# Heads' probabilities turned by transposing transfers of 2-byte halves instead of products with the unit matrix

## The chip, the cores and the metric

The kernel runs on one core of a Trainium2 chip. Five engines work side by side, each through its own queue of instructions in order: TensorE (PE; its weight loads are listed apart as PEld), VectorE (DVE), ScalarE (ACT), GpSimd (POOL) and SyncE (SP), which here only issues transfers. They wait for each other through semaphores. The metric is the device time of one execution in microseconds (us); the median of the runs shown counts.

## The reference

A trunk of two layers over 256 tokens of width 2048, batch 1, all in float32: a Mamba-2 layer, then a sparse-attention layer, each followed by `x <- LayerNorm(alpha * x + mixer(x))`. The change lies in the second layer, in the attention of its 32 heads:

```python
c_q, c_kv, k_idx, w_idx, gate = jnp.split(proj, [s1, s2, s3, s4], -1)
q = (c_q @ w_uq).reshape(b, L, DSA_N_HEADS, DSA_HEAD_DIM)
q_lat = jnp.einsum('bthd,hcd->bthc', q, w_uk)
...
_, sel = lax.top_k(score, k_top)                  # 64 of up to 256 keys for each token
kv_sel = jax.vmap(lambda c, i: c[i])(c_kv, sel)
logits = jnp.einsum('bthc,btkc->bthk', ql, kv_sel) * attn_scale
logits = jnp.where(valid[:, :, None, :], logits, -jnp.inf)
pr = jax.nn.softmax(logits, -1)
return jnp.einsum('bthk,btkc->bthc', pr, kv_sel)  # then: @ w_uv per head, * silu(gate), @ w_out
```

The kernel does not gather. It makes full keys and values of each head (`k`, `v`), adds a mask `mb` that drops the keys outside the chosen 64, and takes the softmax over all causal keys.

## The kernel before

Weights come in units of 128x1024 float32 (512 KB). `Stream.load` lets SP load one into one of four `raw` buffers; `Stream.convert` and `finish` split it into a rounded part `hi` (ACT, L120) and a rest `lo` (DVE, L144), again four buffers each, three to four units ahead of PE; each product on PE is then done as hi*hi + hi*lo + lo*hi. `Stream.run` sets the order of everything: for each unit it emits the conversion of a later one, the unit's own products on PE, and then one step of every active side job. A side job is a Python generator, and each `yield` ends its step for this unit. A step that stands k yields after another is thus k units later in every engine's queue; the tile pools add the waits that buffers and data need.

The heads' stage takes two heads (a pair `p`) after each other from units `pair_a` (keys and values, L956 to L967) and `pair_b` (queries, L978 to L980), with one or two gate products of two units each in between (L336, `g`). `head_steps(h)` is the side job of one head. Token rows lie on the 128 partitions, in two halves, and only causal blocks are kept, so a head's scores are 128x384: a first block of 128 for the earlier half and 256 for the later. Its steps, one unit each:

1. four products of queries and keys into `pl` (L1016 to L1019)
2. DVE adds the mask, scales and takes the row maximum (L1027) into `lg`
3. ACT takes the exponential and the row sum (L1032)
4. DVE divides by the sum (L1035, L1037)
5. nothing
6. PE turns the three 128x128 blocks of `lg` with `ident` into PSUM, `pt` (L1043)
7. ACT copies the first 256 columns, rounded, into `ph` (L1049) and the last 128 into `p2` (L1050); DVE takes the rest `pl` (L1051)
8. nothing
9. PE multiplies values and turned probabilities (L1055 to L1058)
10. to 12. DVE multiplies with the gate into `og` (L1061), then ACT and DVE split it (L1068, L1070)

`lg` and `og` have two buffers each. A period of the stage is ten units with four heads: two units lie between one head's start and the next, three times, and then four. `cmask` is a 128x384 mask that the first layer used; `par` holds per-channel parameters, whose first 256 columns the first layer used. GpSimd does no arithmetic in the heads' stage.

Of the kernel before, what the change touches and what calls it, by code (L numbers as in the profile page):

```python
# [9 lines left out]
F32 = mybir.dt.float32  # L10
F32R = mybir.dt.float32r
I32 = mybir.dt.int32
AF = mybir.ActivationFunctionType
ALU = mybir.AluOpType
PSUM = bass.MemoryType.PSUM

P = 128
T = 256
# [51 lines left out]
class Stream:  # L70
# [30 lines left out]
    def convert_halves(self, i):  # L101
# [3 lines left out]
        for k in range(2):  # L105
            c = slice(k * 512, (k + 1) * 512)
            self.nc.scalar.activation(h[:, c], r[:, c], AF.Copy)
            self.nc.vector.tensor_sub(l[:, c], r[:, c], h[:, c].bitcast(F32))
        self.ready += 1

    def convert(self, i, eng, later=False):

        if i < len(self.units):
# [4 lines left out]
            if u.use in (KEYS, TWO):  # L118
                r = r.rearrange("p (a b) -> p a b", a=2)
            self.nc.scalar.activation(h, r, AF.Copy)  # L120
            self.halfway[i] = l, r, h.bitcast(F32)
# [56 lines left out]
def trunk_kernel(ctx: ExitStack, tc: tile.TileContext, x, xt, w1, wdt, dtp, prm, wo1,  # L178
                 wkv, wcq, wix, wg, wab, wo2, lnr, out):
    nc = tc.nc  # L180
# [18 lines left out]
    def y_tile(name):  # L199
        return p_y.tile([P, 512], F32, tag="y", name=name)  # L200

    def m_tile(name):
        return p_m.tile([P, 512], F32, tag="m", name=name)
# [9 lines left out]
    par = cpool.tile([P, PC_N], F32, tag="par", name="par")  # L213
# [3 lines left out]
    ident = cpool.tile([P, P], F32, tag="ident", name="ident")  # L217
    make_identity(nc, ident)
    cmask = cpool.tile([P, 384], F32, tag="cmask", name="cmask")
# [6 lines left out]
    def rsqrt(pool, dst, val, n, w, tag):  # L226

        t = pool.tile([n, w], F32, tag=tag, name=tag)
        v.tensor_scalar(dst.bitcast(I32), val.bitcast(I32), -0.5, MAGIC, op0=ALU.mult,
                        op1=ALU.add)  # L230
# [5 lines left out]
    def rsqrt1_steps(dst, val, t):  # L236

        v.tensor_scalar(dst.bitcast(I32), val.bitcast(I32), -0.5, MAGIC1, op0=ALU.mult,
                        op1=ALU.add)
# [35 lines left out]
    def dt_steps():  # L275
# [3 lines left out]
        da, acs = (scr[0:NH1, 6144 + T * k:6144 + T * (k + 1)] for k in range(2))  # L279
        nc.scalar.activation(x0, p_dt[:, 0:P], AF.Identity, bias=dtb[:, 0:1])  # L280
        nc.scalar.activation(an, dtb[:, 1:2], AF.Exp)
        v.scalar_tensor_tensor(e, x0, -1.0, x0, op0=ALU.mult, op1=ALU.min)
        v.tensor_scalar_mul(an, an, -1.0)
        nc.scalar.activation(e, e, AF.Exp)
        v.tensor_scalar_add(s, e, 2.0)
# [99 lines left out]
    def conv_steps(g, kind, ci, cc, cell):  # L385
# [4 lines left out]
        def w(k):  # L390
            return convh[:, cc * 5 + k:cc * 5 + k + 1]
        nc.scalar.activation(acc, ps, AF.Identity, scale=w(3), bias=w(4))
        yield
# [187 lines left out]
    for g in range(NG):  # L581
        for kind, n in (("B", 1), ("C", 1), ("x", 4), ("z", 4)):
            for ci in range(n):
# [5 lines left out]
                for half in range(2):  # L589
                    k = len(st.units)  # L590
# [420 lines left out]
    def head_steps(h):  # L1011
        p, k = divmod(h, 2)
        (qh, ql, q1), (kh, kl, k1) = ([a[:, k, :] for a in PR[p][nm]] for nm in "qk")
        vh, vl, v2 = (a[:, k * P:(k + 1) * P] for a in PR[p]["v"])
        pl = y_tile(f"lg{h}")
        nc.tensor.matmul(pl[:, 128:384], qh, kh, start=True, stop=False)  # L1016
        nc.tensor.matmul(pl[:, 128:384], qh, kl, start=False, stop=False)
        nc.tensor.matmul(pl[:, 128:384], ql, kh, start=False, stop=True)
        nc.tensor.matmul(pl[:, 0:128], q1, k1, start=True, stop=True)  # L1019
        yield  # L1020
        lg = d2.tile([P, 384], F32, tag="lg", name=f"lgs{h}")
        mx = d2.tile([P, 2], F32, tag="mx", name=f"mx{h}")
        sm = d2.tile([P, 2], F32, tag="sm", name=f"sm{h}")
        rn = d2.tile([P, 2], F32, tag="rn", name=f"rn{h}")
        parts = ((0, 0, 128), (1, 128, 384))
        for j, a, b in parts:
            v.tensor_tensor_reduce(out=lg[:, a:b], in0=pl[:, a:b], in1=mb[:, a:b],  # L1027
                                   scale=-ATT_SCALE, scalar=3.0e38, op0=ALU.add, op1=ALU.min,
                                   accum_out=mx[:, j:j + 1])
        yield  # L1030
        for j, a, b in parts:
            nc.scalar.activation(lg[:, a:b], lg[:, a:b], AF.Exp, scale=-1.0,  # L1032
                                 bias=mx[:, j:j + 1], accum_out=sm[:, j:j + 1])
        yield
        v.reciprocal(rn, sm)  # L1035
        for j, a, b in parts:
            v.tensor_scalar(lg[:, a:b], lg[:, a:b], rn[:, j:j + 1], 0.5,  # L1037
                            op0=ALU.mult, op1=ALU.mult)
        yield
        yield  # L1040
        pt = m_tile(f"pt{h}")
        for a in (0, 128, 256):
            nc.tensor.transpose(pt[:, a:a + 128], lg[:, a:a + 128], ident)  # L1043
        yield
        if h == 0:
            d2.tile([P, 48], F32, tag="gap3", name="gap3", bufs=1)
        ph, pl = (d2.tile([P, T], F32R, tag=f"prT{j}", name=f"prT{h}_{j}") for j in range(2))
        p2 = d2.tile([P, P], F32, tag="prT2", name=f"prT{h}_2")
        nc.scalar.activation(ph, pt[:, 0:T], AF.Copy)  # L1049
        nc.scalar.activation(p2, pt[:, T:384], AF.Copy)  # L1050
        v.tensor_sub(pl, pt[:, 0:T], ph.bitcast(F32))  # L1051
        yield
        yield
        po = y_tile(f"o{h}")
        nc.tensor.matmul(po[:, 0:T], vh, ph, start=True, stop=False)  # L1055
        nc.tensor.matmul(po[:, 0:T], vh, pl, start=False, stop=False)
        nc.tensor.matmul(po[:, 0:T], vl, ph, start=False, stop=False)
        nc.tensor.matmul(po[:, P:T], v2, p2, start=False, stop=True)  # L1058
        yield
        og = d2.tile([P, T], F32, tag="og", name=f"og{h}")  # L1060
        v.tensor_mul(og, po[:, 0:T], GT.pop(h))  # L1061
        if h == 0:
            OG.append(big.tile([P, KT, 2 * T], F32R, tag="A", name="og0"))
        if h == 16:
            OG.append(big.tile([P, KT, 2 * T], F32R, tag="C", name="og1"))
        dst = OG[h // 16][:, h % 16, :]
        yield
        nc.scalar.activation(dst[:, 0:T], og, AF.Copy)  # L1068
        yield
        v.tensor_sub(dst[:, T:2 * T], og, dst[:, 0:T].bitcast(F32))  # L1070
        yield
# [3 lines left out]
    for p in range(NH2 // 2):  # L1075
        src = wab[2 * p]
        i = st.add(wab[2 * p], 1024, pair_a(p), KEYS)
        st.side(i, (evac_steps, p, ("k", "v")))
        i = st.add(wab[2 * p + 1], 1024, pair_b(p), STILL)
        st.side(i, (evac_steps, p, ("q",)))  # L1080
        if p == 0:
            st.extra[i + 1] = 64
        st.side(i + 3, (head_steps, 2 * p))
        st.side(i + 5, (head_steps, 2 * p + 1))
        n = (left * (p + 1)) // 16 - (left * p) // 16
        for _ in range(n):
            add_gate(next(gates))
# [146 lines left out]
    d2 = L["d2"] = heads.enter_context(tc.tile_pool(name="d2", bufs=2))  # L1234
# [110 lines left out]
    for i in range(len(st.units) - 4, len(st.units)):  # L1345
        st.homes[i] = wmore, 0
    wturn = ctx.enter_context(tc.tile_pool(name="wturn", bufs=1))
    turned = [[cqT[:, n, :], (cqT[:, 3, :], ckvT[:, 0, :], ckvT[:, 1, :])[n]]
              for n in range(3)] + [wturn.tile([P, P], F32R, tag="idr", name="idr")]
# [95 lines left out]
```

## Time and profile before

| | |
|---|---|
| median of 3 runs | 1222.63 us (1221.64 to 1222.91) |
| the profiled execution | 1221.88 us, its span 1219.9 us |
| granted TensorE clock, mean | 0.999 |
| heads' stage (797 to 1053 us of the span) | 256 us |
| transposes of the heads (L1043) | 96, from 797.0 to 1050.1 us |
| weight loads (L98) | 512 KB each, landing 3.5 to 4.0 us after issue (medians) |

A row of the timeline reads: start, duration, engine, line, operation, output <- inputs, sizes, count. A row of groups gives count, busy time, mean nanoseconds of one. Matmuls are pipelined, so the durations of neighbours overlap; the chain of waits counts each stretch of time once.

### The profile page before, as it was taken

What the parts mean: (1) busy time and instruction counts of PE and PEld (TensorE: products, weight loads), DVE (VectorE), ACT (ScalarE), POOL (GpSimd) and SP (SyncE); (2) the same over time, 40 slices, a digit from 0 to 9 for tenths busy, and PEclk for the clock granted to TensorE, in tenths of its full rate; (3) what the DMA queues carried; (4) which work ended last, traced back from release to release, by engine and by line L of the source; (5) the groups of instructions that cost most, each with busy time, mean ns of one, the idle gap of its engine ahead of it and who ended that gap; (6) DMA issues with size and microseconds to landing.
All of it is one profiled execution on the core that took longest, in us unless ns stands there. A gap on an engine that the chain in (4) does not pass through costs nothing.

```text
span 1219.9 us, 22898 instructions
## 1 busy us (share of the span) xinstructions
PE 1213.8 (99%) x8983; PEld 1132.3 (93%) x8983; DVE 907.1 (74%) x1651; ACT 670.8 (55%) x1178; POOL 71.2 (6%) x109
## 2 busy tenths in 40 slices
PE   9999999999999999999999999999999999999998
PEld 8999999999999999788888899999999999888886
DVE  6978788898888788757457768867777777566467
ACT  5555555666566556444346655566666666434341
POOL 0001011101110110110000000000000001000000
PEclk9999999999999999999999999999999999999999
DMA  8656656576656665566556564655544455876662
GB/s 299 217 200 187 207 189 205 166 228 194 201 171 226 195 196 178 194 246 220 190 191 200 202 206 153 178 159 165 159 160 152 156 161 193 314 230 184 198 192 100
DMA packets 65628, 236.78 MB, mean 194 GB/s; under 512 B 8024, under 2 KB 8160, under 8 KB 65136
## 3 DMA queue, kind: packets, MB, share of 16 engines
q1 hardware_dynamic: 60608, 215.29, 53.7%
q0 software_dynamic: 4912, 20.02, 5.1%
q8 instruction: 71, 1.16, 0.4%
q14 instruction: 37, 0.30, 0.1%
HBM read 231.00 MB, written 4.28 MB: 193 GB/s over the span
## 4 chain that ended last, share of the span: by engine, by line
PE 98%; DMA 1%; DVE 0%; issue 0%; SPq 0%; ACT 0%; DVEq 0%
PE acc L336 35%; PE g L336 14%; PE o L615 9%; PE o L617 9%; PE o L616 9%; PE y L494 2%; PE q L978 1%; PE q L979 1%; PE q L980 1%; PE pt L1043 1%; DMA scr<-in_xt_dram 1%; PE k L956 1%; PE k L957 1%; PE k L958 1%; PE v L967 1%; PE v L965 1%
## 5 line engine op out<-in xcount | busy, mean ns | idle before, releaser
L144 DVE TENSOR_TENSOR lo<-raw,hi 128x1024 fp32r<-128x1024 f32 (+1 forms) x400 | 489.1, 1225 | 256.6 <-ACT hi L120 256.2
L120 ACT ACTIVATE hi<-raw 128x1024 fp32r<-128x1024 f32 (+1 forms) x400 | 418.2, 1051 | 209.1 <-PE o L617 154.6
L336 PE MATMUL acc<-xT,hi 128*128 128x256 f32 (+1 forms) x2496 | 301.2, 277 | 0.0
L336 PEld LDWEIGHTS acc<-xT,hi 128*128 128x128 f32 x2496 | 291.1, 188 | 2.5 <-ACT E L447 1.2
L336 PE MATMUL acc<-xT,lo 128*128 128x256 f32 (+1 forms) x1248 | 156.6, 277 | 0.0
L336 PEld LDWEIGHTS acc<-xT,lo 128*128 128x128 f32 x1248 | 148.2, 188 | 0.1
L336 PE MATMUL g<-x1T,hi 128*128 128x256 f32 (+1 forms) x1024 | 126.4, 278 | 0.0
L336 PEld LDWEIGHTS g<-x1T,hi 128*128 128x128 f32 x1024 | 120.4, 188 | 0.2
L615 PE MATMUL o<-hi,yg 128*128 128x512 f32 x256 | 100.3, 392 | 0.0
L615 PE MATMUL o<-hi,og 128*128 128x512 f32 (+1 forms) x256 | 99.7, 389 | 0.0
L617 PE MATMUL o<-hi,yg 128*128 128x512 f32 x256 | 99.7, 389 | 0.0
L616 PE MATMUL o<-lo,yg 128*128 128x512 f32 x256 | 99.6, 389 | 0.0
L617 PE MATMUL o<-hi,og 128*128 128x512 f32 (+1 forms) x256 | 98.9, 386 | 0.0
L616 PE MATMUL o<-lo,og 128*128 128x512 f32 (+1 forms) x256 | 98.8, 386 | 0.0
L336 PE MATMUL g<-x1T,lo 128*128 128x256 f32 x512 | 70.2, 281 | 0.0
L396 DVE SCALAR_TENSOR_TENSOR ca<-acc,par,ca 128x255 f32<-128x255 f32 x138 | 66.2, 479 | 3.3
L336 PEld LDWEIGHTS g<-x1T,lo 128*128 128x128 f32 x512 | 62.9, 188 | 0.2
L403 ACT ACTIVATE xs<-ca 128x256 f32<-128x256 f32 x32 | 13.4, 419 | 83.0 <-DVE ca L396 49.5
L615 PEld LDWEIGHTS o<-hi,yg 128*128 128x128 f32 x256 | 48.1, 188 | 10.3 <-issue 0.2
L617 PEld LDWEIGHTS o<-hi,yg 128*128 128x128 f32 x256 | 48.0, 188 | 9.9
L616 PEld LDWEIGHTS o<-lo,yg 128*128 128x128 f32 x256 | 48.1, 188 | 9.8
L617 PEld LDWEIGHTS o<-hi,og 128*128 128x128 f32 x256 | 48.0, 188 | 9.8
(296 smaller groups left out, 1744.1 us busy)
## 6 DMA issues: line engine op xcount, KB each, us to landing
raw<-in_w_dram SPq DMA_DIRECT2D x160, 512.0 KB, 4.0
raw<-in_wo_dram SPq DMA_DIRECT2D x128, 512.0 KB, 4.0
raw<-in_wg_dram SPq DMA_DIRECT2D x64, 512.0 KB, 3.5
raw<-in_wab_dram SPq DMA_DIRECT2D x32, 512.0 KB, 3.8
abc<-acs_d POOLq DMA_DIRECT2D x32, 256.0 KB, 4.5
raw<-in_wcq_dram SPq DMA_DIRECT2D x8, 512.0 KB, 4.4
raw<-in_wkv_dram SPq DMA_DIRECT2D x8, 336.0 KB, 3.0
scr<-in_xt_dram SPq DMA_DIRECT2D x4, 512.0 KB, 6.9
```

Source lines behind the costliest of these rows:

```text
L120: self.nc.scalar.activation(h, r, AF.Copy)
L144: eng.tensor_sub(*self.halfway.pop(i))
L336: nc.tensor.matmul(ps[:, 0:n], wt, xs[:, kt, c * T:c * T + n], start=(kt == 0 and not lo and c == 0), stop=last and c == (1 - lo), skip_gr ...
L396: v.scalar_tensor_tensor(acc[:, d:], ps[:, :T - d], w(k), acc[:, d:], op0=ALU.mult, op1=ALU.add)
L403: nc.scalar.activation(dst, acc, AF.Tanh)
L494: nc.tensor.matmul(py[ks, c * T + s * P:(c + 1) * T], xsT[:, s, c, ks], ms[c][k][:, ws], start=(c == 0 and s == 0), stop=(s == 1), skip_gr ...
L615: nc.tensor.matmul(ps, ah, hs, start=(kk == 2 * first), stop=False)
L616: nc.tensor.matmul(ps, ah, ls, start=False, stop=False)
L617: nc.tensor.matmul(ps, al, hs, start=False, stop=(kk == 31))
L956: nc.tensor.matmul(ps, h[:, 0, o:o + P], ckvT[:, ct, 0:T], start=(ct == 0), stop=False)
L957: nc.tensor.matmul(ps, h[:, 0, o:o + P], ckvT[:, ct, T:2 * T], start=False, stop=False)
L958: nc.tensor.matmul(ps, l[:, 0, o:o + P], ckvT[:, ct, 0:T], start=False, stop=(ct == 1))
```

## The change

Steps 4 to 7 of a head turn the probabilities in another way. A 4-byte word is seen as two 2-byte halves (`bitcast(U16)`). After DVE's division, GpSimd copies `lg` into `cmask` with all low halves first and all high halves behind them (384 each), and SP issues one `dma_start_transpose` that turns the six 128x128 blocks of halves into a new tile `ptu`. Two units later GpSimd joins the halves of the first 256 columns to words, `pt` in SBUF; a unit after that ACT and DVE read these as they read PSUM before, and ACT joins the last 128 columns itself, into a piece of `par`. `ptu` and `ptf` have one buffer, `cmask` is one, and `og` has one buffer instead of two.

```diff
         for j, a, b in parts:
             v.tensor_scalar(lg[:, a:b], lg[:, a:b], rn[:, j:j + 1], 0.5,
                             op0=ALU.mult, op1=ALU.mult)
-        yield
-        yield
-        pt = m_tile(f"pt{h}")
-        for a in (0, 128, 256):
-            nc.tensor.transpose(pt[:, a:a + 128], lg[:, a:a + 128], ident)
+        halves = cmask.bitcast(U16)
+        turned = d2.tile([P, 768], U16, tag="ptu", name=f"ptu{h}", bufs=1)
+        nc.gpsimd.tensor_copy(halves.rearrange("p (a t) -> p a t", a=2),
+                              lg.bitcast(U16).rearrange("p (t a) -> p a t", a=2))
+        nc.sync.dma_start_transpose(turned.rearrange("p (k t) -> p k t", k=6), halves)
+        yield
+        yield
+        pt = d2.tile([P, T], F32, tag="ptf", name=f"ptf{h}", bufs=1)
+        nc.gpsimd.tensor_copy(pt.bitcast(U16).rearrange("p (t a) -> p a t", a=2),
+                              turned.rearrange("p (a t) -> p a t", a=2)[:, :, 0:T])
         yield
...
-        p2 = d2.tile([P, P], F32, tag="prT2", name=f"prT{h}_2")
+        p2 = par[:, P * k:P * (k + 1)]
         nc.scalar.activation(ph, pt[:, 0:T], AF.Copy)
-        nc.scalar.activation(p2, pt[:, T:384], AF.Copy)
+        nc.scalar.activation(p2.bitcast(U16).rearrange("p (t a) -> p a t", a=2),
+                             turned.rearrange("p (a t) -> p a t", a=2)[:, :, T:384], AF.Copy)
         v.tensor_sub(pl, pt[:, 0:T], ph.bitcast(F32))
...
-        og = d2.tile([P, T], F32, tag="og", name=f"og{h}")
+        og = d2.tile([P, T], F32, tag="og", name=f"og{h}", bufs=1)
```

What moves in the queues, at three places. The lines of the changed kernel are one higher up to the edit and seven higher behind it.

PE's queue before, at the end of a pair's query products, where one head is turned (`pt`) between them and a gate product (`g`); `o` is the output product of the head before:

```order
L980 MATMUL q_10217<-cqT,lo_10061 128x256
L1043 MATMUL pt_10243<-ident,lgs_10053 128x128 x3
L336 MATMUL g_10268<-x1T,hi_10105 128x256 x16
L336 MATMUL g_10268<-x1T,lo_10106 128x256 x8
L1055 MATMUL o_10293<-prT_0_10185,hv_0_9714 128x256
L1056 MATMUL o_10293<-prT_1_10186,hv_0_9714 128x256
```

And the same place now:

```order
L981 MATMUL q_10220<-cqT,lo_10064 128x256
L337 MATMUL g_10272<-x1T,hi_10108 128x256 x16
L337 MATMUL g_10272<-x1T,lo_10109 128x256 x8
L1062 MATMUL o_10297<-prT_0_10189,hv_0_9717 128x256
L1063 MATMUL o_10297<-prT_1_10190,hv_0_9717 128x256
```

The three transposes are gone, and nothing else moves on PE.

SP's queue before, over four units; in brackets the waits that stand at an issue (DMAHW: an earlier transfer of SP's, whose semaphore it shares; DVE: the split that frees the buffer):

```order
L98 DMA raw_10021<-in_wab_dram 128x1024 [waits DMAHW0_49,DVE_49]
L98 DMA raw_10064<-in_wab_dram 128x1024 [waits DMAHW1_49,DVE_49]
L98 DMA raw_10109<-in_wg_dram 128x1024 [waits DMAHW2_49,DVE_49]
L98 DMA raw_10156<-in_wg_dram 128x1024 [waits DMAHW3_49,DVE_49]
L98 DMA raw_10215<-in_wg_dram 128x1024 [waits DMAHW4_49,DVE_49]
```

And now, with the transposing transfers of two heads:

```order
L99 DMA raw_10021<-in_wab_dram 128x1024 [waits DMAHW3_49,DVE_49]
L1044 DMA_TRANSPOSE ptu_10053<-cmask 128x6x128 [waits DMAHW4_49,Pool_49]
L99 DMA raw_10067<-in_wab_dram 128x1024 [waits DMAHW5_49,DVE_49]
L99 DMA raw_10112<-in_wg_dram 128x1024 [waits DMAHW6_49,DVE_49]
L1044 DMA_TRANSPOSE ptu_10146<-cmask 128x6x128 [waits DMAHW1_49,Activation_49,Pool_49]
L99 DMA raw_10160<-in_wg_dram 128x1024 [waits DMAHW7_49,DVE_49]
```

Each transfer waits for GpSimd's split, and three of four also for ACT, which must have read the last block of the head before out of `ptu`; the loads behind it wait with it.

POOL's queue had no instruction in the heads' stage and now holds this, two for each head (`cmask` the split, `ptf` the join):

```order
L1048 COPY ptf_10141<-ptu_10053 128x2x256 [waits DMAHW1_49,Activation_49]
L1042 COPY cmask<-lgs_10149 128x768 [waits DVE_49,Pool_49]
L1048 COPY ptf_10246<-ptu_10146 128x2x256 [waits DMAHW4_49,DVE_49]
L1042 COPY cmask<-lgs_10254 128x768 [waits DVE_49,Pool_49]
L1048 COPY ptf_10341<-ptu_10251 128x2x256 [waits DMAHW7_49,DVE_49]
```

A head's split stands behind the join of the head before, and that join behind its transfer.

More of the change, by code (lines that the diff above doesn't have):

```diff
@@ L12 @@
 I32 = mybir.dt.int32
+U16 = mybir.dt.uint16
 AF = mybir.ActivationFunctionType
```

## The prediction

> **What bounds the kernel now.** First the page: its span, the busy table and the chain that ended last.
>
> ```profile
> span 1219.9 us, 22898 instructions
> PE 1213.8 (99%) x8983; PEld 1132.3 (93%) x8983; DVE 907.1 (74%) x1651; ACT 670.8 (55%) x1178; POOL 71.2 (6%) x109
> PE 98%; DMA 1%; DVE 0%; issue 0%; SPq 0%; ACT 0%; DVEq 0%
> ```
>
> TensorE is the bound: 99% busy, and 98% of the chain. An average can hide a stage with another limit, so next come the stretches of the heads' stage, the only one that the change touches. Columns: the stretch, its length, then busy time of PE, weight loads, DVE, ACT and POOL, granted clock, DMA share, GB/s.
>
> ```profile
> 797.00:1053.00 256.00, 255.70 (x2157) 251.82 (x2157) 185.04 (x441) 163.07 (x395) 3.19 (x6) 1.00 0.54 177
> 807.26:840.54 33.28, 33.28 (x294) 33.28 (x294) 24.68 (x59) 20.94 (x53) 0.00 (x0) 1.00 0.50 156
> ```
>
> The stage lasts 256 us. The second row is one period of it, four heads (ten weight units) in 33.28 us, 8.32 us a head. In it PE never pauses, DVE idles 8.60 us, ACT 12.34 us, POOL does nothing, and the DMA engines are half free. What is taken from PE here comes off the end, as long as the other engines still deliver in time.
>
> How long do they have? The chain of waits prices what is removed (start, length, what), and the timeline shows when one head's pieces run.
>
> ```profile
> 909.86 0.33 PE pt L1043 x3
> 916.80 0.33 PE pt L1043 x3
> 930.38 0.33 PE pt L1043 x3
> 936.75 0.33 PE pt L1043 x3
> ...
> 904.90 0.55 DVE L1037 TENSOR_SCALAR lgs<-lgs,rn 128x128 f32<-128x128 f32 x2
> 907.61 0.38 ACT L1049 ACTIVATE prT<-pt 128x256 fp32r<-128x256 f32 x1
> 907.87 0.28 ACT L1050 ACTIVATE prT<-pt 128x128 f32<-128x128 f32 x1
> ...
> 911.91 0.37 ACT L1049 ACTIVATE prT<-pt 128x256 fp32r<-128x256 f32 x1
> 913.26 0.42 DVE L1051 TENSOR_TENSOR prT<-pt,prT 128x256 fp32r<-128x256 f32 x1
> ...
> 919.60 0.19 PEld L1055 LDWEIGHTS o<-prT,hv 128*128 128x128 f32 x1
> ```
>
> Read this as one head: its probabilities are normalised by 905.45 (L1037), turned on PE at 909.86, split on ACT from 911.91 and on DVE until 913.68, and used by PE at 919.60. ACT's slot thus comes 6.46 us after the normalising, and PE needs the result 5.92 us after DVE has it. The ACT rows at 907.61 and 907.87 belong to the head before.
>
> **The change, part by part.** *Removed.* Three transposes a head; the chain gives 0.33 us for the three, in each of the four rows above. 32 heads x 0.33 = 10.5 us of the path. The group's busy time would read 15.7 us, but matmuls overlap, so the chain's figure is the one that counts:
>
> ```profile
> L1043 PE MATMUL pt<-ident,lgs 128*128 128x128 f32 x96 | 15.7, 272 | 0.0
> ```
>
> *Added on the way from L1037 to ACT's slot:* a GpSimd split S of 768 2-byte elements a partition, a transposing transfer T of 192 KB issued by SP, a GpSimd join J of 512 elements. The nearest rows:
>
> ```profile
> L1218 POOL COPY sC<-sC 128x384 f32<-128x384 f32 x1 | 0.5, 503 | 0.1
> L511 POOL TENSOR_TENSOR sq<-sq,sq x8: 1147/1200/1532, 87.2 to 498.5; 128x256 f32<-128x256 f32 x8
> raw<-in_wab_dram SPq DMA_DIRECT2D x32, 512.0 KB, 3.8
> out_dram<-fin SPq DMA_DIRECT2D x8, 256.0 KB, 2.3
> acs_d<-scr POOLq DMA_DIRECT2D x1, 64.0 KB, 2.1
> gb_hk<-in_lnr_dram POOLq DMA_DIRECT2D x8, 256.0 KB, 10.7
> ms_d<-msv POOLq DMA_DIRECT2D x4, 2.0 KB, 1.6
> ```
>
> S and J: no row copies 2-byte elements. By the one-input copy, 503 ns for 384 elements, S is 768/384 x 503 = 1.01 us and J 512/384 x 503 = 0.67 us. Below, half of it, should two halves go through as one word: 0.50 and 0.34. Above, the two-input rate, 1200 ns for 256: 3.6 and 2.4. I take the copy, since both are one-input copies.
>
> POOL and DVE also hold each other up when both read SBUF. One place shows it:
>
> ```profile
> 115.65 2.53 POOL L515 TENSOR_TENSOR sq<-sq,sq 128x256 f32<-128x256 f32 x2 [16.97 <-ACT sq L508]
> 115.82 1.77 DVE L144 TENSOR_TENSOR lo<-raw,hi 128x1024 fp32r<-128x1024 f32 x1
> L144 DVE TENSOR_TENSOR lo<-raw,hi x400: 852/1225/1768, 19.1 to 1195.5; 128x1024 fp32r<-128x1024 f32 x131, 128x672 fp32r<-128x672 f32 x3
> ```
>
> The DVE split that began inside a GpSimd instruction took 1.77 us, 0.55 above its median of 1.225. I add that 0.55 to S and to J each. For DVE itself the worst is that each POOL copy stops it for its whole length, 4 x 1.68 = 6.7 us a period, under its 8.60 us of idle time: nothing on the path, if only this happens.
>
> T: no transposing transfer exists in the trace. Below stands the 256 KB write that SP issues, 2.3 us; above, the slowest transfer of that size, 10.7 us. I take 4.0 us: next to the 3.8 us of the weight loads, since T rides their queue, often behind one, and moves fewer bytes in finer pieces.
>
> *The loop.* One buffer each for split halves, turned halves and joined words makes the heads a ring. SP may not start T of a head before ACT has copied the previous head's second block (it takes L1050's place), and POOL's split of the next head stands behind the join of this one. A turn of the ring is the longer of S (1.01 + 0.55) and ACT's two copies (907.61 to 908.15, 0.54), then T, then J (0.67 + 0.55): 1.56 + T + 1.22 = T + 2.8 us, so 6.8 at T = 4.0. A period without its transposes has 33.28 - 4 x 0.33 = 31.96 us, 8.0 a head. The ring keeps up while T is under 5.2 us, and the time stays flat below that; above it each us of T costs 32 us.
>
> *Inside a period the heads are uneven.* The tightest is the head above: T waits until 908.15, ACT's slot is at 911.91, 3.76 us later; T + J = 5.2 makes ACT 1.5 us late. Behind the waiting ACT queue the key copies (L1005) and the weight splits (L120); DVE's L1051 waits on ACT. PE has 5.92 us in hand there, and ACT makes it good from its 12.34 us of idle time: cost 0.
>
> *The SP queue.* Behind a waiting T stand the weight loads. They wait for DVE's next split anyway:
>
> ```profile
> SPq L98 <- DVE lo L144: 718.8, 281, 8.1
> L98 SPq DMA_DIRECT2D raw<-in_wab_dram x32: 327/328/328, 750.1 to 994.7; - x32
> ```
>
> A load costs SP 0.33 us, and SP waits most of its time. T of the tight head goes out by 908.2; the next load follows the DVE split after it, so little is pushed back: 0. If T's issue holds SP for some us, loads land later; they are issued about four units before use, and 3.8 us of that is needed.
>
> *The rest.* ACT reads joined words from SBUF instead of PSUM, and its second copy writes 256 2-byte elements in place of 128 words: by the rows of 256 and 128 elements some 0.1 us a head more, inside ACT's idle time. The single output buffer adds no wait, since DVE finishes one head's L1070 before it starts the next one's L1061. On POOL's queue two issues of the last stage's loads now stand between a split and its join, some 0.5 us each and once: their wait for the last gate product ends before that join is due. The weights' conversion is untouched.
>
> *Sum.* -10.5 + 0. The profiled execution took 1221.88 us (1219.9 us of span and 2.0 around it); 1221.88 - 10.5 = 1211.4. The median shown, 1222.63, is 0.75 above it, so the forecast against it is 1212.1 us. A measurement of this kernel tells changes from 0.2%, 2.4 us, on.
>
> **The rivals.** *A: the ring becomes the bound, because the transfer is slower than a plain one.* Place: T, between SP's issue and POOL's join; it decides from T = 5.2 us on. If the 192 KB go as three times 64 KB one after another, each at the 2.1 us of that row, T = 6.3, and the time is 1212.1 + 32 x (6.3 - 5.2) = 1247 us. For it: finer pieces, and DMA engines half busy with loads. Against: the 256 KB write lands in 2.3 us.
>
> *B: six blocks of 128x128, each as a transfer of its own.* At the smallest transfer's 1.6 us each, T = 9.6 and the time 1212.1 + 32 x 4.4 = 1353 us. For it: the destination is six blocks. Against: it is one instruction, and the 1.6 us is mostly the way there and back, which one instruction pays once.
>
> The Trainium skill speaks for this rival: its page "VectorE: DVE Perf Modes", section "The three transpose paths", gives 1309 ns for a 128x128 2-byte transpose by DMA against 390 ns on TensorE. Six in a row would be an estimated 7.9 us by that page and about 1298 us in all. No run here shows yet whether the blocks add up, and its 390 ns, for one transpose by itself, is not what the path pays in this trace: 0.11 us (0.33 for three).
>
> *C: GpSimd's 2-byte copies go at its two-input rate.* S = 3.6, J = 2.4 and the same waits: 4.15 + 4.0 + 2.95 = 11.1 us a turn, 3.1 over 8.0, so 1212.1 + 32 x 3.1 = 1311 us.
>
> *D: no change.* The ring runs at 8.3 us a turn (T = 5.5), and the late ACT takes back the 10.5 us: 1222. This needs T in a narrow strip.
>
> **How the numbers follow.** Forecast 0.60, A 0.20, B 0.08, C 0.06, D 0.06. T under 5.2 is likelier than not because both rows on SP's queue, 2.3 and 3.8 us, lie under it. Faster is the forecast alone, 0.60; same is D, 0.06; slower A, B and C, 0.34. The forecast's own range is 1210 to 1217: below, the full 10.5 us and the spread of the three runs, 1.3 us (1221.64 to 1222.91); above, half of the gain lost at the uneven heads. The whole range goes to 1308, T of 8.2 us by the same formula, which takes in A and D and leaves out B and C, 0.14 together.
>
> **What would show it.** Right: the chain without L1043 and still 98% PE, the period near 32.0 us, T landing within 5 us of its issue, POOL busy some 54 us more (32 x 1.68), DVE's splits now and then above 1.3 us. Wrong: PE waiting at the output product for ACT's or DVE's probabilities, ACT waiting long for POOL's join, the period stretched to four times S + T + J; then the time follows T. If T is in bounds and PE waits all the same, my reading of the slack between ACT's slot and PE is what failed.

## The result, and the profile after

The changed kernel takes 1238.53 us (median of 4 runs, 1237.62 to 1239.31), the kernel before 1222.14 us beside it (1221.56 to 1222.91): a ratio of 1.0133, interval [1.0116, 1.0151]. It is 16.4 us slower, where 10.5 us less was forecast. The page, with the lines that answer to those of before:

```profile
span 1237.6 us, 22921 instructions
PE 1212.9 (98%) x8887; PEld 1127.6 (91%) x8887; DVE 919.4 (74%) x1651; ACT 675.6 (55%) x1178; POOL 132.3 (11%) x173
PE 87%; DVE 6%; ACT 4%; DMA 2%; issue 1%; SPq 0%; POOL 0%; DVEq 0%; ACTq 0%; POOLq 0%
```

PE had 98% of the chain and now has 87%; DVE and ACT hold 10%. PE is still "98% busy" over the whole span, so the loss has to be looked for in the heads' stage. Two periods of it (each from the first output product of one head to that of the head four later; heads 4, 8 and 12), in the columns of the stretches:

```profile
840.53:875.65 35.12, 32.82 (x283) 32.29 (x282) 26.68 (x60) 22.20 (x53) 8.56 (x8) 1.00 0.59 173
875.65:910.31 34.66, 32.83 (x283) 32.30 (x282) 26.05 (x60) 22.19 (x53) 7.71 (x8) 1.00 0.62 175
```

A period had 33.28 us with PE never idle. It now has 34.7 to 35.1, of which PE is idle for about 2. DVE has 1.4 to 2.0 us more to do a period, ACT 1.25 more. What PE waits for (in all, times, longest):

```profile
PE o L1062 <- DVE og L1068: 10.7, 7, 1.9
PE o L1062 <- ACT prT L1055: 4.2, 1, 4.2
PE o L1062 <- DVE rn L1036: 1.9, 6, 0.3
PE lg L1017 <- DVE mx L1028: 1.8, 6, 0.3
```

The first line is the surprise. The output product of a head does not wait for its probabilities. It waits for `og`, DVE's gate product of the head *before*. Logits and output products share a PSUM pool of two buffers (`y_tile`), and the next output product can only be written when `og` has read the previous one. The second line happens once, near the end of the stage.

The new pieces themselves are quick (transfer: time to issue, count and landing; GpSimd's split and join):

```profile
L1044 SPq DMA_TRANSPOSE ptu<-cmask x32: 1217/1217/1983, 793.1 to 1068.0; - x32
DMA to landing us min/median/max: 2.5/2.6/15.3
...
L1042 POOL COPY cmask<-lgs 128x768 uint16<-128x768 uint16 x32 | 32.6, 1018 | 206.9 <-DVE mx L1028 116.4 <-DVE lgs L1038 90.4
L1048 POOL COPY ptf<-ptu 128x512 uint16<-128x512 uint16 x32 | 29.2, 912 | 125.7 <-DMA ptu<-cmask 110.9 <-DVE hv L995 6.7 <-DVE lo L145 4.4
```

The landing median is 2.6 us; the one of 15.3 us belongs to the second line of the waits.

Now the same place in both timelines, the head that the prediction called the tightest. First the kernel before:

```profile
917.70 0.42 DVE L1070 TENSOR_TENSOR og<-og,og 128x256 fp32r<-128x256 f32 x1
918.04 0.42 DVE L1061 TENSOR_TENSOR og<-o,sC 128x256 f32<-128x256 f32 x1
```

`og` (L1061) ended at 918.46, and PE's output product began at 919.60 (a row shown in the prediction): a margin of 1.14 us. After:

```profile
917.12 1.22 DVE L145 TENSOR_TENSOR lo<-raw,hi 128x1024 fp32r<-128x1024 f32 x1
918.25 1.04 DVE L1058 TENSOR_TENSOR prT<-ptf,prT 128x256 fp32r<-128x256 f32 x1
...
922.18 1.62 DVE L145 TENSOR_TENSOR lo<-raw,hi 128x1024 fp32r<-128x1024 f32 x1 [0.53 <-ACT hi L121]
923.73 0.41 DVE L1077 TENSOR_TENSOR og<-og,og 128x256 fp32r<-128x256 f32 x1
924.24 0.42 DVE L1068 TENSOR_TENSOR og<-o,sC 128x256 f32<-128x256 f32 x1
...
917.33 1.69 POOL L1042 COPY cmask<-lgs 128x768 uint16<-128x768 uint16 x1 [0.49 <-DVE lgs L1038]
922.01 0.77 POOL L1048 COPY ptf<-ptu 128x512 uint16<-128x512 uint16 x1 [2.99 <-DMA ptu<-cmask]
...
924.81 0.36 PE L1062 MATMUL o<-prT,hv 128*128 128x256 f32 x1 [1.63 <-DVE og L1068]
```

DVE's rest of the probabilities (L1058) took 1.04 us beside GpSimd's split, against 0.42 before; a weight split took 1.62 beside GpSimd's join, against 1.23. Between L1077 and `og` there is now a gap of 0.10 us, where before they overlapped. The margin is used up, and PE stands for 1.63 us.

### The profile page after: what moved, and what is told of

It is laid out like the page before. It is cut to its first block, busy times and chain, and to the rows that moved or that the text cites. A ratio compares the mean times of both kernels' runs of the same rounds, so it can differ in the third digit from the quotient of the medians.

```text
span 1237.6 us, 22921 instructions
## 1 busy us (share of the span) xinstructions
PE 1212.9 (98%) x8887; PEld 1127.6 (91%) x8887; DVE 919.4 (74%) x1651; ACT 675.6 (55%) x1178; POOL 132.3 (11%) x173
## 4 chain that ended last, share of the span: by engine, by line
PE 87%; DVE 6%; ACT 4%; DMA 2%; issue 1%; SPq 0%; POOL 0%; DVEq 0%; ACTq 0%; POOLq 0%
PE acc L337 35%; PE g L337 9%; PE o L616 9%; PE o L617 9%; PE o L618 9%; DVE lo L145 2%; PE y L495 2%; ACT hi L121 2%; DMA ptu<-cmask 1%; PE q L979 1%; PE q L981 1%; PE q L980 1%; DVE lgs L1028 1%; DMA scr<-in_xt_dram 1%; ACT lgs L1033 1%
## 5 line engine op out<-in xcount | busy, mean ns | idle before, releaser
L145 DVE TENSOR_TENSOR lo<-raw,hi 128x1024 fp32r<-128x1024 f32 (+1 forms) x400 | 494.4, 1238 | 250.4 <-ACT hi L121 250.1
L404 ACT ACTIVATE xs<-ca 128x256 f32<-128x256 f32 x32 | 13.4, 419 | 82.9 <-DVE ca L397 49.5
L618 PEld LDWEIGHTS o<-hi,og 128*128 128x128 f32 x256 | 48.5, 189 | 10.1
L617 PEld LDWEIGHTS o<-lo,og 128*128 128x128 f32 x256 | 48.5, 189 | 9.8
L616 PEld LDWEIGHTS o<-hi,og 128*128 128x128 f32 x256 | 48.6, 190 | 9.6
L616 PEld LDWEIGHTS o<-hi,yg 128*128 128x128 f32 x256 | 48.1, 188 | 10.2 <-ACT hi L121 0.2
```

Of the source, the lines that this page charges most:

```text
L145: eng.tensor_sub(*self.halfway.pop(i))
L404: nc.scalar.activation(dst, acc, AF.Tanh)
L616: nc.tensor.matmul(ps, ah, hs, start=(kk == 2 * first), stop=False)
L617: nc.tensor.matmul(ps, ah, ls, start=False, stop=False)
L618: nc.tensor.matmul(ps, al, hs, start=False, stop=(kk == 31))
```

## The experiments

The theories. *L*: GpSimd's reads of SBUF make DVE's instructions late. *B*: the single `og` buffer does. *C*: ACT and DVE form a chain that is nearly as long as PE's work, so that whatever is taken from PE alone can't pay, and whatever is added to ACT or DVE comes out at the end. *T*: the transfer, its issue on SP or the loads beside it. Each time stands against the kernel before on the same chip, 1222.15 to 1222.4 us; ratios are given with their intervals. Some of the kernels leave something out and serve as measurements alone: e1 and e5 to e8 take a constant for the turned probabilities, e2 and e11 leave them unturned, e3 and e15 turn a constant. A "period" in the text is the mean over heads 7 to 27, from the starts of their output products (five periods; 33.40 us before, 35.15 after).

**One side of the change alone (e1).** The kernel before without the 96 products:

```diff
-        pt = m_tile(f"pt{h}")
-        for a in (0, 128, 256):
-            nc.tensor.transpose(pt[:, a:a + 128], lg[:, a:a + 128], ident)
+        pt = cmask
```

> The kernel before without the 96 transposes and with nothing in their place: ACT and DVE read a constant 128x256 tile of SBUF instead of the turned probabilities, so the output product leaves the probabilities out. It prices the removal alone. Theory L (what eats the gain is GpSimd reading SBUF beside DVE's two-input instructions, which makes DVE late) and theory B (the single output buffer og does it) both expect the full gain, 1222.1 - 10.5 = 1211.6 us, period of four heads 31.95 us. Theory C (the chain of ACT and DVE in this stage is itself about as long as PE's work, so that PE has nothing to gain) expects 1219 to 1223 us and a period of 33.0 us or more, with PE waiting at the output product.

Measured: 1219.33 us, 0.9977 [0.9968, 0.9987]. Of 10.5 us, 2.8 came off, and the period is still 33.34. So even without any added work the removal hardly pays, as C expected and L and B did not. PE's waits in the heads' stage of this kernel:

```profile
PE lg L1016 <- DVE mx L1027: 2.0, 7, 0.3
PE o L1053 <- DVE og L1059: 1.0, 1, 1.0
```

Both are waits for a reader in the shared PSUM pool: the row maximum reads the logits, `og` the output product.

**The change without the transfer (e2:** `turned = halves`, ACT's second copy from a constant**), and without GpSimd's reads (e3:** its copies become fills of `cmask` and `pt` with 0.5**):**

> The changed kernel without its 32 transposing transfers: GpSimd splits and joins as before, but the join reads the split halves unturned, and ACT's second copy reads a constant, so the probabilities enter unturned. Theory L expects the changed kernel's period of about 35.1 us to stay (DVE splits of 1.4 to 1.6 us beside GpSimd's copies), and only the collision of the last heads' transfer with the 4 MB of the last stage's loads, 6.4 us, to go: 1238.5 - 6.4 = 1232 us. A rival T (the transfer: its 1.2 us on SP and its share of the DMA engines push the weight loads back) expects the period to fall to 32 to 33 us, 1212 to 1222 us in all. Theory B expects 1232 too, since og still has one buffer.

> The changed kernel with GpSimd's two copies of each head replaced by memsets of the same tiles, which write SBUF and read nothing; transfers, buffers and waits between join, ACT and SP stay. The probabilities are left out (a constant is turned). Theory L expects DVE's weight splits back at 1.22 us and L1058 at 0.42, the period at 32 to 33 us, and the time at 1238.5 - 8 x 2.5 = about 1218 us with the collision at the end still in. Theory B and theory C expect the period to stay near 35 us and the time at 1234 to 1239.

Measured: 1228.54 us, 1.0054 [1.0039, 1.0069], and 1227.49 us, 1.0051 [1.0035, 1.0068]. Both lie between the ranges that the theories gave. e2 has no transfer, and so nothing of its own in the way of the last stage's loads (e4), and it is still 9.2 us over e1: the transfer is not the whole loss. e3 is 11.0 us under the changed kernel and 8.2 over e1, but its slowest transfer still lands in 13.4 us, so it does not tell what is left besides the reads.

**The last stage's loads later (e4)**, behind the last transfer, and with them the job that uses them:

```diff
-    st.run(n_heads)
+    st.run(n_heads + 6)
...
-    st.side(n_heads + 7, (x1_steps,))
+    st.side(n_heads + 15, (x1_steps,))
```

> The changed kernel with the two 2 MB loads of the last stage issued six units later, behind the last head's join on GpSimd's queue, and the steps that use them eight units later. If the 15.3 us landing of head 29's transfer is that collision, it lands in 2.6 us, PE's wait of 4.2 us at its output product and the halved clock behind it go, and the time is 1238.5 - 6.4 = 1232 us. If it is not, 1238.5 stays. Theories L, B and C agree on this one.

Measured: 1231.56 us, 1.0081 [1.0066, 1.0096]; the slowest transfer lands in 4.5 us instead of 15.3, where 2.6 was expected. So 7.0 us of the 16.4 are one event. In the changed kernel the chain shows it, with GpSimd's queue and the loads' landing times ahead:

```profile
1044.46 0.54 POOL L1346 DMA_DIRECT2D fin<-x_d  x1
1044.99 0.53 POOL L1348 DMA_DIRECT2D fin<-in_lnr_dram  x1
...
fin<-x_d POOLq DMA_DIRECT2D x1, 2048.0 KB, 10.3
fin<-in_lnr_dram POOLq DMA_DIRECT2D x1, 2048.0 KB, 14.8
...
1045.15 15.26 DMA ptu<-cmask
...
1061.79 0.58 PE o L1062
...
1063.59 0.43 PE o L616
...
1067.36 0.23 PE o L616
```

Head 29's transfer of 192 KB starts with 4 MB of loads and ends with them. PE waits 4.2 us, and then its products take 0.43 us instead of 0.23 until 1067 us; the granted clock of the stretch from 1061 to 1072 us is 0.72.

**Where does the removal's gain go?** The turned probabilities' PSUM buffers (`m_tile`) are free now. Four kernels, each e1 with one edit more:

```diff
-        po = y_tile(f"o{h}")
+        po = m_tile(f"o{h}")                                             # e5
...
-        og = d2.tile([P, T], F32, tag="og", name=f"og{h}")
+        og = d2.tile([P, T], F32, tag="og", name=f"og{h}", bufs=1)       # e6
...
+        for a in (0, 192):                                               # e7
+            nc.gpsimd.tensor_copy(par[:, 0:192]..., lg[:, a:a + 192]...)
+        nc.gpsimd.tensor_copy(par[:, 0:T]..., lg[:, 0:T]...)             # e7, two units later
...
-        nc.scalar.activation(p2, pt[:, T:384], AF.Copy)
+        nc.scalar.activation(p2.bitcast(U16)..., pt[:, T:384].bitcast(U16)..., AF.Copy)   # e8
```

> The kernel before without the 96 products that turn the probabilities (a constant in SBUF stands for the turned ones), and now the output product of a head writes to the two PSUM buffers that the turned probabilities had, instead of sharing the two buffers of the logits. Without the second part the removal gained only 2.8 of 10.5 us. If the gain was lost because PE waits for DVE's product og to free a PSUM buffer, that wait goes and the time falls to 1212 to 1215 us, with PE's waits on og near nothing. If the chain of ACT and DVE itself is as long as PE's remaining work (theory C), the waits reappear at the logits' product (for mx) or at the probabilities, and the time stays at 1217 to 1220.

> The kernel before without the 96 products, as above but with the output product where it was, and with one buffer for og instead of two. If the single buffer matters (theory B), DVE's product og now waits for the last reader of the head before and the time rises from 1219.3 to 1222 us or more. If not, it stays within 1218.3 and 1220.3.

> The kernel before without the 96 products, and with three copies of 2-byte halves on GpSimd a head (1280 elements in all, as in the changed kernel), whose results nobody reads. Nothing waits for them, except the buffer of the logits two heads on. If GpSimd's reads beside DVE are what makes DVE late (theory L), the time rises by 3 to 6 us over 1219.3, to 1222.5 to 1225.5, and DVE's mean for the splits L144 grows. If they cost nothing, 1218.3 to 1220.3.

> The kernel before without the 96 products, and with ACT's copy of the last 128 probabilities done in 2-byte halves (256 elements, 0.49 us for 0.28 us) as in the changed kernel. If ACT stands in the chain that sets the period, the 0.21 us a head come to 6.7 us at most and the time rises from 1219.3 to 1221 to 1226. If ACT has slack, 1218.3 to 1220.3.

| kernel | us | ratio | against 1219.33 |
|---|---|---|---|
| e5, output product in buffers of its own | 1212.78 | 0.9923 [0.9910, 0.9935] | -6.6 |
| e6, one `og` buffer | 1222.12 | 1.0000 [0.9991, 1.0008] | +2.8 |
| e7, GpSimd's reads, for nobody | 1222.53 | 1.0003 [0.9994, 1.0012] | +3.2 |
| e8, ACT's longer copy | 1222.33 | 1.0000 [0.9991, 1.0009] | +3.0 |

Each edit lies in the range of the theory that blamed it, and none is the whole. In e7 DVE's splits take 1276 ns in the mean for 1224 in e5. The three costs add up: 1219.33 + 2.8 + 3.2 + 3.0 = 1228.3, and the kernel with all three (the change without the transfer) had 1228.54 (e2). With PSUM buffers of its own for the output product, neither it nor the logits' product waits, PE is full again, and the period is 32.35 us:

```profile
PE g L336 <- DVE gate L803: 0.4, 1, 0.4
...
797.00:1055.00 258.00, 257.56 (x2115) 251.83 (x2114) 188.89 (x445) 169.03 (x402) 3.20 (x6) 1.00 0.56 183
```

So the first reading of C, that the chain of ACT and DVE is by itself as long as PE's work, is wrong in this form. It becomes long by the PSUM buffer, which ties PE's next product to `og`.

**Is the PSUM buffer then the whole story?** The changed kernel with that edit, with the late loads (e9) and without (e10):

> The changed kernel whole, with two edits: the output product of a head writes to the two PSUM buffers that the turned probabilities had, and the 4 MB of the last stage's loads start some 12 us later, behind the last transposing transfer. If the three costs that take 2.8 to 3.2 us each (single og buffer, GpSimd's reads, ACT's longer copy) and the transfer's 3 us all reach PE only through the PSUM buffer that DVE's product og frees, all go and the time is 1212 to 1214 us, 8 to 10 us under the kernel before. If they reach PE in another way too (the probabilities come late by themselves), it stays at 1217 to 1222, with PE's waits on ACT's or GpSimd's work.

> The changed kernel whole with the PSUM edit alone; the loads of the last stage start where they did. If the collision of head 29's transfer with these loads is a cost of its own, it takes some 4 to 7 us more than the kernel with both edits: 1216 to 1221 us. If the freed PSUM buffer gives the transfer the slack that it needs, within 1 us of it.

Measured: 1228.07 us, 1.0053 [1.0039, 1.0066], and 1238.15 us, 1.0131 [1.0117, 1.0145]. Neither time lies in a range that was expected for it. The freed buffer gives only 3.5 us (1231.56 to 1228.07), and with the early loads nothing: the collision then costs 10.1 us. The period of e9 is 34.92 us. The wait has moved to another PSUM buffer, that of the gate products, which DVE frees too:

```profile
PE g L337 <- DVE gate L804: 9.6, 10, 1.9
PE g L337 <- DVE sC L804: 1.6, 1, 1.6
```

One such place, in this kernel (ACT, DVE, GpSimd, PE):

```profile
841.23 0.39 ACT L1008 ACTIVATE hq<-q 128x256 f32<-128x256 f32 x1 [3.40 <-DVE hq L1007]
...
842.76 0.49 ACT L1056 ACTIVATE par<-ptu 128x256 uint16<-128x256 uint16 x1
...
843.98 1.05 ACT L121 ACTIVATE hi<-raw 128x1024 fp32r<-128x1024 f32 x1
...
845.06 1.23 DVE L145 TENSOR_TENSOR lo<-raw,hi 128x1024 fp32r<-128x1024 f32 x1 [0.90 <-ACT hi L121]
...
848.33 1.04 DVE L1058 TENSOR_TENSOR prT<-ptf,prT 128x256 fp32r<-128x256 f32 x1
849.29 0.41 DVE L804 SCALAR_TENSOR_TENSOR sC<-sC,g 128x256 f32<-128x256 f32 x1
...
847.40 1.69 POOL L1042 COPY cmask<-lgs 128x768 uint16<-128x768 uint16 x1 [0.49 <-DVE lgs L1038]
...
849.85 2.12 PE L337 MATMUL g<-x1T,hi 128*128 128x256 f32 x16 [1.60 <-DVE sC L804]
```

And the same pieces in e5, which has no added work:

```profile
838.57 0.38 ACT L1007 ACTIVATE hq<-q 128x256 f32<-128x256 f32 x1 [2.81 <-DVE hq L1006]
...
840.10 0.30 ACT L1048 ACTIVATE prT<-cmask 128x128 f32<-128x128 f32 x1
...
845.53 0.42 DVE L1049 TENSOR_TENSOR prT<-cmask,prT 128x256 fp32r<-128x256 f32 x1
845.87 0.41 DVE L803 SCALAR_TENSOR_TENSOR sC<-sC,g 128x256 f32<-128x256 f32 x1
```

Read it as one chain: ACT waits for DVE (`hq`), then works without a pause until `hi`; DVE waits for `hi`, then works without a pause until the gate; PE waits for the gate. From ACT's `hq` copy to the gate's end it takes 8.47 us here (841.23 to 849.70) and 7.71 us in e5 (838.57 to 846.28). The 0.76 us are the two additions: 0.14 until ACT's `hi` starts, behind its copy of 0.49 us for 0.30, and 0.62 on DVE, 1.04 for 0.42. Each of the engines is idle for a quarter of the time or more, but they are idle in turn, each while the other works. On such a chain no addition to either is hidden.

**Which of the additions, and the transfer?** All with the output product's own buffers. e11 is the change without transfers; the others are the kernel of 1228.07 us with one edit or both (with the edit of `og` the later heads' gates get eight buffers instead of seven, which no run separates from it):

```diff
-        p2 ... nc.scalar.activation(p2..., turned...[:, :, T:384], AF.Copy)
+        nc.gpsimd.tensor_copy(p2..., turned...[:, :, T:384])             # e14, e12: behind the join
...
-        og = d2.tile([P, T], F32, tag="og", name=f"og{h}", bufs=1)
-        v.tensor_mul(og, po[:, 0:T], GT.pop(h))
+        og = GT.pop(h)                                                   # e13, e12
+        v.tensor_mul(og, po[:, 0:T], og)
```

> The changed kernel without the transposing transfers (the halves are joined as they are; ACT's copy of the last 128 reads a constant), and with the output product in the PSUM buffers that the turned probabilities had. GpSimd's copies, ACT's copy in halves and the single og buffer stay. If the transfer is what made 1228.1 of 1212.8, the time is 1212 to 1215 us. If the copies lengthen the chain of ACT and DVE beyond PE's 32 us for four heads, 1222 to 1228, with PE's gate product waiting for DVE's gate.

> The changed kernel with the output product in the freed PSUM buffers and the last stage's loads late (1228.1 us as measured), and two more edits: GpSimd instead of ACT joins the last 128 probabilities (ACT has 0.49 us a head less, GpSimd some 0.4 more), and og is made in the gate's own buffer, so that nothing waits for the single og buffer. If the chain of ACT and DVE sets the period, it falls by up to 0.5 us a head towards PE's floor: 1213 to 1220 us, under the kernel before. If GpSimd's longer reads cost DVE as much as ACT gains, or the probabilities' path by the transfer is the limit, 1225 to 1230.

> As e12 but with og in the gate's buffer alone; ACT still joins the last 128. If the single og buffer is part of the chain here as it was in e6 (2.8 us), 1224 to 1226.5; if it is not, 1227 to 1229.

> As e12 but with GpSimd's join of the last 128 alone; og keeps its single buffer. If ACT's 0.49 us a head stands in the chain and GpSimd's added read blocks DVE for less, 1216 to 1224; if the one pays for the other, 1226 to 1230.

Measured: e11 1226.18 us, 1.0033 [1.0020, 1.0045]: the transfer is worth 1.9 us here; the other 13.4 us over e5 stay without it (GpSimd's copies, ACT's longer copy and the single `og` buffer). e13 1225.12, 1.0025 [1.0016, 1.0033]: the `og` buffer is worth 2.95 us, as before. e14 1224.07, 1.0017 [1.0009, 1.0026]: ACT's copy is worth 4.0 net, although GpSimd reads more for it. e12, both: 1221.49, 0.9996 [0.9987, 1.0005], level with the kernel before and between its two expectations. What DVE's instructions of two SBUF inputs take in it (count, busy, mean ns), and in e5:

```profile
L145 DVE TENSOR_TENSOR lo<-raw,hi 128x1024 fp32r<-128x1024 f32 x78 | 102.7, 1317 | 41.0 <-ACT hi L121 41.0
...
L1058 DVE TENSOR_TENSOR prT<-ptf,prT 128x256 fp32r<-128x256 f32 x32 | 18.6, 580 | 0.0
...
L1077 DVE TENSOR_TENSOR og<-sC,og 128x256 fp32r<-128x256 f32 x16 | 8.3, 517 | 0.0
```

```profile
L144 DVE TENSOR_TENSOR lo<-raw,hi 128x1024 fp32r<-128x1024 f32 x80 | 98.0, 1224 | 54.1 <-ACT hi L120 54.1
...
L1049 DVE TENSOR_TENSOR prT<-cmask,prT 128x256 fp32r<-128x256 f32 x32 | 13.4, 419 | 0.0
L1068 DVE TENSOR_TENSOR og<-og,og 128x256 fp32r<-128x256 f32 x31 | 13.0, 419 | 0.0
```

In this stretch, 797 to 1055 us, GpSimd adds 93 ns to a split (78 x 0.093 = 7.3 us), 161 to the probabilities' rest (32 x 0.161 = 5.2), and 98 to the rest of `og` in the row shown (16 x 0.098 = 1.6). Is that the remaining 8.7 us over e5? e15 fills instead of copying. And if the chain is what limits, a kernel that loads it for half the heads only and turns the others on PE should be faster than both: e16 and e17 (`by_dma = h % 4 < 2`, `by_dma = h % 2 == 1`).

> As e12 (1221.5 us), but GpSimd's three copies a head are fills of the same areas with a constant: they write and read nothing, so that the output is not the reference's; the transfer and all waits stay. If GpSimd's reads beside DVE make the rest of the loss (theory L), 1212.5 to 1215.5 us, and DVE's mean for the splits L145 goes from 1.31 to 1.23 us. If the transfer or its waits make it, 1219 to 1222.

> As e12, but only two heads of four (h mod 4 = 0 and 1) go by the transfer; the other two are turned by PE as in the kernel before, with their output product in the logits' buffers. PE loses 16 x 0.33 = 5.3 us of work, its floor is 1217 us. If the chain of ACT and DVE was a little longer than PE's period only because of what the 32 transfers add to it, half of that fits: 1217 to 1219. If the two kinds of heads hinder each other (one PSUM pool shared by turned probabilities and output products), 1220 to 1224.

> As e16, but the odd heads go by the transfer. The same floor; by the explanation with the chain 1217 to 1219, and the difference from e16 tells whether it matters which heads they are. By the rival 1220 to 1224.

e15 takes 1211.55 us, 0.9912 [0.9899, 0.9926], 1 us below the range that theory L gave and far from the rival's, and PE waits for nothing in this stretch:

```profile
797.00:1070.00 273.00, 273.00 (x2191) 265.09 (x2191) 198.24 (x457) 169.04 (x377) 30.28 (x99) 1.00 0.76 210
...
L145 DVE TENSOR_TENSOR lo<-raw,hi 128x1024 fp32r<-128x1024 f32 x80 | 97.9, 1224 | 50.9 <-ACT hi L121 50.9
```

DVE's splits are back at 1224 ns and PE is never idle. One reservation: a fill does not wait for the probabilities, so that the ring's start is loosened too, which the expectation did not say; the 9.9 us between e12 and e15 are the reads and that together. The waits of e12 bound the second part: in the heads' stage ACT waits for GpSimd's join twice, 2.9 us in all, and neither PE, DVE nor the conversion of the weights waits for a join or a transfer. So by these rows some 7 of the 9.9 us or more are the reads. The transfer stays in e15, with a median landing of 4.6 us, and costs PE nothing there. e16 takes 1219.86 us, 0.9981 [0.9972, 0.9990], e17 1220.85, 0.9990 [0.9981, 0.9999]: e16 is the fastest that leaves nothing out, 18.7 us under the changed kernel and 2.3 under the one before, though 0.9 above what was expected of it, between its two ranges. e17 lies in the range of its rival: in it PE waits 3.8 us for the logits' maxima on DVE, in e16 0.6, so it matters which heads they are.

## Why the prediction was wrong

The measured steps make a ladder from the time that was forecast to the one that came:

| kernel | us | step |
|---|---|---|
| e15: no products, transfers with fills | 1211.55 | |
| e12: GpSimd copies instead of filling | 1221.49 | +9.9 |
| e9: ACT's join and the single `og` buffer | 1228.07 | +6.6 |
| e4: the output product in the shared PSUM buffers | 1231.56 | +3.5 |
| the changed kernel: the loads beside head 29's transfer | 1238.53 | +7.0 |

The steps hold in this order. Taken in another place they differ: the PSUM buffers are worth 6.6 us from e1 to e5 and 3.5 here.

What held:

- *Removed, 10.5 us.* e15 is 10.6 under the kernel before, e5 9.5.
- *T, taken as 4.0 us.* It is 2.6, near its lower bound. The ring's turn is thus 2.6 + 2.8 = 5.4 us by the prediction's formula, under the 8.0 a head, and rivals A and B, which priced a slow T, did not happen. For B the Trainium skill ("VectorE: DVE Perf Modes", section "The three transpose paths") gave 1309 ns for a block, and the estimate from it was 7.9 us for six in a row; six in one instruction land in 2.6 us, so they do not add up.
- *S and J.* GpSimd's busy time rose by 61.1 us (71.2 to 132.3) where 54 was forecast; rival C's rate is out.

What failed, each a place where a cost was put at nothing:

- *"PE has 5.92 us in hand there ... cost 0."* The slack was read on one path, from the head's own probabilities. PE's output product has a second release, the PSUM buffer that `og` of the previous head frees, and there the margin was 1.14 us. e5 shows it: with own buffers the gain of the removal is 9.5 us instead of 2.8, the waits of the logits' product in the same pool included. This is the step that the prediction named for the case that T is in bounds and PE waits all the same.
- *"6.7 us a period, under its 8.60 us of idle time: nothing on the path, if only this happens."* The bound on the blocking was right: by the rows of e12 the splits, the probabilities' rest and the row of `og`'s rest lose 7.3 + 5.2 + 1.6 us in 258, or 1.8 us a period. The idle time was not free: it is DVE's wait for ACT within a chain. GpSimd's reads for nobody cost 3.2 us (e7), and some 7 to 9.9 in the change (e12 against e15).
- *ACT "some 0.1 us a head more, inside ACT's idle time".* It is about 0.2 us, and outside: it cost 3.0 us in e8. In e14, where ACT's whole copy of 0.49 us goes, 4.0 us come off.
- *"The single output buffer adds no wait."* The gap between L1077 and `og` is 0.10 us, where the two had overlapped; it costs 2.8 us (e6) and 2.95 (e13).
- *The two issues of the last stage's loads, "some 0.5 us each and once".* The issues took 0.54 and 0.53 us. Their 4 MB in flight beside one transfer were not counted: 7.0 us.

None of the rivals held a wait of this kind; the slower cases were all slow transfers or slow copies, and the one narrow case D (no change) needed them too. That the blocking is a matter of GpSimd's reads agrees with the Trainium skill, page "SBUF — State Buffer", section "Who interferes with whom": a DVE instruction with two SBUF inputs contends with a GpSimd instruction that reads SBUF, and not with one that only writes it. The rows agree: splits of 1317 ns beside copies, 1224 beside fills.

Still open is how the 9.9 us divide exactly between the reads and the loosened start of the ring: the waits of e12 leave the second at most 2.9 of them, but a kernel with the waits of the copies and none of their reads was not tried.

## What to carry to other kernels

Before calling an engine's idle time slack, ask what ends it: where ACT waits for DVE and DVE for ACT in turn, both are idle for much of the time, and what is added to either can come out at the end. For each product on the bounding engine list every release, the PSUM buffer's last reader as well as the operands, and take the smallest margin; here the operands had 5.92 us and the buffer 1.14. When work leaves the bounding engine, look at what the freed buffers can do: they were worth 6.6 us to e5, more than twice what the removal alone gave.

## What was not expected of the hardware

- In the profiled execution of the changed kernel the granted clock was 0.50 twice within the heads' stage (columns of the stretches as above):

```profile
961.34:964.73 3.39, 3.39 (x18) 3.39 (x17) 1.56 (x2) 3.39 (x10) 0.00 (x0) 0.50 0.34 95
1060.33:1067.14 6.81, 5.35 (x14) 4.29 (x15) 3.71 (x7) 5.14 (x12) 3.32 (x4) 0.50 0.81 245
```

  The first stretch began 1.1 us after a wait of PE of 1.9 us had ended, the second 2.7 us into the wait of 4.2 us. Waits of up to 1.7 us left the clock at 1.00, and so did one of 1.9 us in e9. The Trainium skill's page "TensorE: Matmul & The Clock Gate", section "Part 1: The HAM clock gate (the "warmup" mystery)", has the clock fall to half after an idle window of some 3.4 us and come back after as long a busy one. The lengths of the two stretches, 3.4 and 6.8 us, fit one and two such windows; the falls do not agree, since PE had stood still for only 1.9 and 2.7 us before them.
- A 192 KB transposing transfer holds SP for 1.22 us (a plain load 0.33), lands in 2.6 us (median in the changed kernel; 4.6 in e15), and in 15.3 when 4 MB of plain loads start beside it.
- GpSimd's blocked split shows its own loss too: 1.69 us against 0.83 undisturbed. In the pair at 847 to 849 us above both engines end late, the one of DVE by 0.62 us.
